# Down weights of two FFNs summed by POOL during the first up projection, and A split six blocks ahead

## The chip, the core and the metric

The kernel runs on one core of one Trainium2 chip. The metric is the device time of one execution in microseconds. Engines are named as the profile names them: PE (matmuls), PEld (PE's weight loads), DVE (the vector engine), ACT (the scalar engine), POOL (GpSimd), SP (the engine that only issues transfers).

## The reference, cut to what matters

Two transformer blocks follow each other on one sequence of 1024 tokens with 1024 features, in float32. Each ends with an FFN of hidden width 2816, and the change touches nothing else:

```python
# block 1
gate, up = jnp.split(xn @ w_gate_up[l], 2, axis=-1)
x = x + (jax.nn.silu(gate) * up) @ w_down[l]
# block 2
u = causal_dwconv(h @ w_ffn_up[l], w_ffn_conv[l])
gate, val = jnp.split(u, 2, axis=-1)
x = x + (jax.nn.silu(gate) * val) @ w_ffn_down[l]
```

## The kernel before, in words

**Precision.** A float32 product is made of three matmuls. Each operand is split into a rounded part "hi" (a copy on ACT, L256) and the rest "lo" (source minus hi on DVE, L257), and PE adds hi·hi, hi·lo and lo·hi (`mm3` at L267 to L269, `product` at L973).

**Up projections.** A unit f (1 to 21) makes 128 hidden features with one level of a Strassen scheme: 7 products of 4 row blocks, so 84 matmuls of 128x512. Its two raw weight blocks of 512 KB (u for up, g for gate) are loaded by SP (L129) into a ring of two raw buffers. Four slots per unit, a to d, are split from them; `add_unit` also forms sums of weight blocks in place on the raw buffers: S3 and S4 on DVE, S1 and S2 on POOL (L878). Slot b needs S3 and S1, slot c S2, slot d S4. A slot is split at most three slots ahead of the one in use, and u and g of the next unit are loaded when the raw buffer before them has been split. The finished hidden features (`sg`) go to DRAM (`hd`, L1059).

**Down projections.** The first 20 of the 22 hidden blocks are a 2x2 Strassen product: A (hidden features, from `hd`) times B (the down weights), in quadrants of 10 blocks. `DOWN` lists the seven products in order: A11·B11, A12·B21, S3·T3, A22·T4, S1·T1, S2·T2, S4·B22. S are sums of quadrants of A, T sums of quadrants of B (T3 = B22-B12, T1 = B12-B11, T2 = B11+T3, T4 = B21-T2). A product is 10 steps; a step is one k block of A for four token tiles, 12 matmuls into four PSUM banks. For every step one block of A must have been split (`operand`, tiles `ah`), in a ring of AR = 3, so three steps ahead at the most. The sums S are formed in `operand` (L1194). B11, B12 and B21 are loaded whole into SBUF at the start (L1142), B22 in pieces twice (L129), and `add_down` forms T3 and T1 on DVE and T2 and T4 on POOL (L845) right before the splits that use them. Finished banks are added to x by DVE (L980, `x<-dn,x`).

**The order of the work.** The program is written in one order, and a scheduler then places every instruction on its engine's queue by its own estimates of when it is ready; each engine runs its queue strictly in that order. So the order of a queue need not be that of the code. A transfer queued on SP behind another one that waits for its buffer waits too.

**Names that the prediction uses.** `wr` raw weights, `wh` and `wl` their split parts, `st` and `dn` PSUM banks of the up and the down projection, `a22` two buffers for quadrant A22, `sg` a finished hidden block, `pb` (new) POOL's ring of down weight blocks, `td` (new) the sums in DRAM.

Of the kernel before, what the change touches and what calls it, by code (L numbers as in the profile page):

```python
# [52 lines left out]
DE = dict(S3=pool_, T3=vec_, T1=vec_, T2=pool_, T4=pool_, S1=vec_, S2=vec_, S4=pool_)  # L53
# [104 lines left out]
class Kern:  # L158
# [6 lines left out]
    def setup(self):  # L165
        tc, nc = self.tc, self.nc
        self.const = c = tc.alloc_tile_pool(name="const", bufs=1)
        self.xnp = tc.alloc_tile_pool(name="xn", bufs=1)
        self.W = Weights(self, tc.alloc_tile_pool(name="w", bufs=1), 2, 3)
        self.dram = tc.alloc_tile_pool(name="dram", bufs=1, space=DRAM)  # L170
        self.hd = self.dram.tile([NF, P, S], F32, name="hd")
        self.ident = c.tile([P, P], F32, name="ident")
# [643 lines left out]
    def plan_ffn(self, which):  # L816
        a, W = self.a, self.W
        up = (a["w_gate_up"] if which == 1 else a["w_ffn_up_2"])[0].rearrange("(k p) c -> p k c", p=P)
        dn = (a["w_down"] if which == 1 else a["w_ffn_down_2"])[0].rearrange("(k p) c -> p k c", p=P)
        units, dw = {}, {}  # L820
        units[0] = [W.add([(0, up[:, :, o:o + P])], KT, P) for o in (0, DFF)]
        for f in range(1, NF):
            units[f] = self.add_unit(*[up[:, :, o + f * P:o + (f + 1) * P] for o in (0, DFF)])
        home, slots = {}, {}

        def rest():
            for f in range(2 * ND, NF):
                dw[f] = W.add([(0, dn[:, f:f + 1, :])], 1, D)

        for _, name in DOWN:  # L830
            if which == 1 and name == "T2":
                rest()
            for k in range(0, ND, 2):
                slots[name, k] = self.add_down(home, name, k, dn)
        if which == 2:
            rest()
        self.ffn_plan[which] = (units, home, slots, dn, dw)

    def add_down(self, home, name, k, dn):

        W, nc = self.W, self.nc
        raw = W.load([(0, dn[:, ND + k:ND + k + 2, 512:])], 2, 512) if name in ("T3", "B22") else None

        def tt(out, in0, in1, what):
            DE[what](nc).tensor_tensor(out=out, in0=in0, in1=in1, op=ALU.subtract)  # L845

        def make(hi, lo):
            out = []
            for j in range(2):
                h, l = (v[:, j * 512:(j + 1) * 512] for v in (hi, lo))  # L850
                b11, b12, b21 = (home.get((q, k + j)) for q in ("B11", "B12", "B21"))
                b22 = None if raw is None else W.raw[raw][:, j * 512:(j + 1) * 512]
                if name == "T3":
                    src = home["T3", j]
                    tt(src, b22, b12, "T3")
                    tt(b12, b12, b11, "T1")
                    tt(b11, b22, b12, "T2")
                else:
                    src = dict(B11=b11, B21=b21, T4=b21, T1=b12, T2=b11, B22=b22)[name]
                    if name == "T4":  # L860
                        tt(b21, b21, b11, "T4")
                self.split(h, l, src)
                out.append((h, l))
            return out
        return W.slot(make, raw)

    def add_unit(self, gate, up):
# [9 lines left out]
        def tt(name, in0, in1, op, what):  # L877
            SE[what](nc).tensor_tensor(out=raw(name), in0=raw(in0), in1=raw(in1), op=op)  # L878
# [63 lines left out]
    def ffn(self, which):  # L942
# [118 lines left out]
        def unit(f):  # L1061
# [32 lines left out]

            if f < NF - 1:
                second()
                third()
                flush(f - 1)
                add(v[:, main], b5, u2[:, main])
            else:  # L1100
                third()
                down_load()
                second()
                flush(f - 1)
                add(v[:, main], b5, u2[:, main])
                W.done(sb)
# [7 lines left out]
            add(u2[:, main], b5, u2[:, main])  # L1114
            if f == NF - 1:
                down_open()
# [19 lines left out]
        def fetch(q, k0, k1):  # L1136

            f = k0 + ND * ((q[2] if q[0] == "A" else q[1]) == "2")
            c = 512 * ((q[1] if q[0] == "A" else q[2]) == "2")
            src = self.hd[f:f + k1 - k0, :, c:c + 512].rearrange("k p c -> p k c") if q[0] == "A" else \  # L1140
                dn[:, f:f + k1 - k0, c:c + 512]
            nc.sync.dma_start(out=places[q, k0][:, :k1 - k0, :], in_=src)  # L1142
# [8 lines left out]
        def down_load():  # L1151

            for q, part in (("A11", "hi0"), ("B11", "lo0")):
                place(q, self.xnp.tile([P, KT, 512], F32, tag=part, name=q), 0, KT)
            for k in range(0, KT, 2):
                fetch("A11", k, k + 2)
                fetch("B11", k, k + 2)
# [3 lines left out]
        def down_open():  # L1161
# [7 lines left out]
            for j in range(2):  # L1169
                home["T3", j] = d.tile([P, 512], F32, name=f"T3{j}")  # L1170
            ring["a22"] = [d.tile([P, 512], F32, name=f"a22{i}") for i in range(A2)]
            for q in ("A11", "B11", "A21", "B12"):
                place(q, d.tile([P, ND - KT, 512], F32, name=f"{q}x"), KT, ND)
            for q, part in (("A21", "hi1"), ("B12", "lo1")):
                place(q, self.xnp.tile([P, KT, 512], F32, tag=part, name=q), 0, KT)
            fetch("A11", KT, ND)
            fetch("B11", KT, ND)
            fetch("A12", 0, ND // 2)
            fetch("A12", ND // 2, ND)
            for i in range(AR):  # L1180
# [39 lines left out]
        def load_rest():  # L1220

            dp.pop().release()
# [8 lines left out]
        def strassen():  # L1231
            pool.release()
            last = None
            d2 = tc.alloc_tile_pool(name=f"dr{which}", bufs=1, side="right", reuse_waits="tile")
            dp.append(d2)
            self.psum(dn=(1, 8))
            place("B21", d2.tile([P, ND, 512], F32, name="B21"), 0, ND)
            for q in ("B21", "A21", "B12"):
                cuts = ((0, ND // 2), (ND // 2, ND)) if q == "B21" else ((0, KT // 2), (KT // 2, KT), (KT, ND))
                for k0, k1 in cuts:  # L1240
                    fetch(q, k0, k1)
            for k in range(A2):
                load22(k)
            sums = []
            for i, (name, bname, k) in enumerate(steps):
# [14 lines left out]
                w = W.get(slots[bname, k - k % 2])[k % 2]  # L1260
# [20 lines left out]
            if which == 1:  # L1281
                W.done(slots[DOWN[-1][1], ND - 2])
            return last
# [3 lines left out]
        pool = tc.alloc_tile_pool(name=f"ffn{which}", bufs=1, side="right", reuse_waits="tile")  # L1287
        first(banks)
# [8 lines left out]
        else:  # L1297
# [3 lines left out]
            dp[1].release()  # L1301
# [956 lines left out]
```

## Time and profile before

| | |
|---|---|
| median of three runs | 2538.17 us (2536.41 to 2547.12) |
| the profiled execution | 2533.62 us |
| its span, first to last instruction | 2531.9 us |
| mean granted clock of PE, share of full speed | 0.986 |
| busy: PE, DVE, ACT, POOL | 96%, 73%, 45%, 18% |
| first up projection | about 500 to 950 us of the span |
| first down projection | about 950 to 1190 us |
| second up projection | about 1840 to 2285 us |
| second down projection | about 2285 to 2515 us |

The profile is of one execution. A busy PE is one with matmuls in its pipeline, so the number of matmuls in a stretch says more than its busy time. A group of instructions is told by its line, its engine and its tiles, and a line can be that of a helper which many stages call.

### The profile page before, as it was taken

How to read it: one execution, taken by the hardware profiler on the slowest of the kernel's cores; microseconds unless marked ns; L12 is line 12 of the kernel's file. 1: busy time of each engine (PE TensorE's matmuls, PEld its weight loads, DVE VectorE, ACT ScalarE, POOL GpSimd, SP SyncE). 2: the span in 40 equal slices, each digit the busy share in tenths (PEclk: the TensorE clock that was granted, in tenths of full speed). 3: DMA queues.
4: the chain of work that ended last, by engine and by line, in shares of the span. 5: the costliest groups of instructions: out<-in, count | busy, mean ns of one | idle time of the engine just before them, and what ended most of it. 6: DMA issues, size and time to landing. Idle time of an engine off the chain costs nothing. (4 is left out here: it accounts for less than half of the span.)

```text
span 2531.9 us, 33317 instructions
## 1 busy us (share of the span) xinstructions
PE 2420.6 (96%) x12360; PEld 1993.5 (79%) x12360; DVE 1856.3 (73%) x3342; ACT 1145.8 (45%) x2290; POOL 449.3 (18%) x412
## 2 busy tenths in 40 slices
PE   7999999999999999899999999989899999999898
PEld 7977779978888887678877777879678888887677
DVE  5557788655555557977777868777878788878977
ACT  5356675342232233337432434776744434434243
POOL 1000002031111114500210111332341111113600
PEclk9999999999999999899999999999999999999999
DMA  4110002112223236213211112131212222227202
GB/s 152 51 34 21 22 26 92 42 48 78 75 83 91 76 110 240 75 42 123 62 42 50 30 46 64 40 137 49 75 51 84 92 75 75 84 93 265 67 33 109
DMA packets 194675, 196.58 MB, mean 78 GB/s; under 512 B 11613, under 2 KB 154032, under 8 KB 194512
## 3 DMA queue, kind: packets, MB, share of 16 engines
q1 hardware_dynamic: 189760, 178.74, 22.2%
q0 software_dynamic: 4752, 15.71, 1.8%
q8 instruction: 97, 1.59, 0.3%
q14 instruction: 66, 0.54, 0.1%
HBM read 155.76 MB, written 38.67 MB: 77 GB/s over the span
## 5 line engine op out<-in xcount | busy, mean ns | idle before, releaser
L257 DVE TENSOR_TENSOR wl<-wr,wh 128x512 fp32r<-128x512 f32 (+4 forms) x388 | 300.9, 805 | 320.1 <-ACT wh L256 316.2
L256 ACT CAST wh<-wr 128x512 fp32r<-128x512 f32 (+4 forms) x388 | 257.2, 696 | 583.4 <-PE st L973 363.9
L269 PE MATMUL dn<-wh,ah 128*128 128x512 f32 x560 | 225.6, 403 | 21.6 <-DVE ah L257 21.6
L267 PE MATMUL dn<-wh,ah 128*128 128x512 f32 x560 | 226.0, 404 | 5.4 <-ACT ah L256 2.2
L268 PE MATMUL dn<-wl,ah 128*128 128x512 f32 x560 | 224.0, 400 | 0.0
L980 DVE TENSOR_TENSOR u<-st,u 128x512 f32<-128x512 f32 x260 | 168.0, 685 | 30.7 <-PE st L973 29.3
L878 POOL TENSOR_TENSOR wr<-wr 128x512 f32<-128x512 f32 x42 | 55.2, 1315 | 692.3 <-DVE wr L878 692.3
L269 PEld LDWEIGHTS dn<-wh,ah 128*128 128x128 f32 x560 | 107.3, 192 | 56.3 <-DVE ah L257 30.8
L973 PE MATMUL st<-f1hi,wl 128*128 128x512 f32 x368 | 147.2, 400 | 0.0
L973 PE MATMUL st<-f2hi,wl 128*128 128x512 f32 x368 | 147.1, 400 | 0.0
L973 PE MATMUL st<-f2lo,wh 128*128 128x512 f32 x368 | 147.0, 400 | 0.0
L973 PE MATMUL st<-f1lo,wh 128*128 128x512 f32 x368 | 146.6, 398 | 0.0
L973 PE MATMUL st<-f1hi,wh 128*128 128x512 f32 x368 | 145.2, 394 | 0.7 <-ACT f1hi L256 0.7
L973 PE MATMUL st<-f2hi,wh 128*128 128x512 f32 x368 | 145.0, 394 | 0.7 <-ACT f2hi L256 0.7
L267 PEld LDWEIGHTS dn<-wh,ah 128*128 128x128 f32 x560 | 107.4, 192 | 32.8 <-ACT ah L256 4.1
L268 PEld LDWEIGHTS dn<-wl,ah 128*128 128x128 f32 x560 | 107.5, 192 | 24.0
L256 ACT CAST ah<-A 128x512 fp32r<-128x512 f32 x104 | 63.7, 619 | 109.7 <-PE dn L268 94.7
L257 DVE TENSOR_TENSOR ah<-A,ah 128x512 fp32r<-128x512 f32 x104 | 82.4, 796 | 41.9 <-ACT ah L256 38.9
L973 PEld LDWEIGHTS st<-f2hi,wh 128*128 128x128 f32 x368 | 70.4, 191 | 17.3 <-ACT f2hi L256 0.9
L973 PEld LDWEIGHTS st<-f1hi,wh 128*128 128x128 f32 x368 | 70.4, 191 | 17.2 <-ACT f1hi L256 0.9
L973 PEld LDWEIGHTS st<-f2lo,wh 128*128 128x128 f32 x368 | 69.6, 189 | 16.0
L973 PEld LDWEIGHTS st<-f1lo,wh 128*128 128x128 f32 x368 | 69.4, 189 | 16.1
(547 smaller groups left out, 7079.8 us busy)
## 6 DMA issues: line engine op xcount, KB each, us to landing
wr<-in_w_gate_up_dram SPq DMA_DIRECT2D x44, 512.0 KB, 4.3
hd<-sg SPq DMA_DIRECT2D x44, 512.0 KB, 3.2
wr<-in_w_ffn_up_dram SPq DMA_DIRECT2D x44, 512.0 KB, 3.9
wr<-in_w_mix_in_dram SPq DMA_DIRECT2D x28, 512.0 KB, 4.0
wr<-in_w_in_dram SPq DMA_DIRECT2D x16, 512.0 KB, 3.9
wr<-in_w_down_dram SPq DMA_DIRECT2D x12, 512.0 KB, 3.3
wr<-in_w_ffn_down_dram SPq DMA_DIRECT2D x12, 512.0 KB, 3.3
A<-hd SPq DMA_DIRECT2D x4, 1280.0 KB, 14.3
```

The source lines that it names most:

```text
L256: self.nc.scalar.copy(hi, src)
L257: self.nc.vector.tensor_tensor(out=lo, in0=src, in1=hi.bitcast(F32), op=ALU.subtract)
L267: mm(out, a[0], b[0], start=start, stop=False)
L268: mm(out, a[0], b[1], start=False, stop=False)
L269: mm(out, a[1], b[0], start=False, stop=stop)
L878: SE[what](nc).tensor_tensor(out=raw(name), in0=raw(in0), in1=raw(in1), op=op)
L973: mm(ps, a[p][:, kk, :], b[q][:, kk, :], start=start and kk == 0 and j == 0, stop=kk == n - 1 and j == 2, skip_group_check=True)
L980: nc.vector.tensor_tensor(out=out, in0=ps, in1=t, op=ALU.add)
```

## The change

POOL forms T1 to T4 of both FFNs during the first up projection. `prepare_down` is a generator; each step of it is called at one of three places in a unit of the first FFN. For each of 20 k blocks (10 of each FFN) SP loads the four blocks B12, B22, B11, B21 (256 KB each) into the ring `pb` of six buffers, POOL makes the four sums in place and stores each (256 KB) to `td` by its own transfer queue: 80 loads, 80 sums, 80 stores. The down projections then take B11, B21, B22 and the T's as ordinary weights through the ring `wr`, 35 loads of 512 KB each, split as one piece of 128x1024. S1 and S2 of the units of the first FFN go from POOL to DVE; in the second FFN they stay. In the down projections S2 goes from DVE to POOL. The ring `ah` has six buffers: three (AR0) where the three were, and three in the memory that the up projection's pool leaves.

```diff
-ND, AR, A2, PB = 10, 3, 2, 2
+ND, AR, AR0, A2, PB = 10, 6, 3, 2, 2
-SE, TE, ME = dict(S3=vec_, S1=pool_, S2=pool_, S4=vec_), dict(T1=vec_, T2=pool_, T3=pool_, T4=pool_), vec_
+SE = {1: dict(S3=vec_, S1=vec_, S2=vec_, S4=vec_), 2: dict(S3=vec_, S1=pool_, S2=pool_, S4=vec_)}
-DE = dict(S3=pool_, T3=vec_, T1=vec_, T2=pool_, T4=pool_, S1=vec_, S2=vec_, S4=pool_)
+DE = dict(S3=pool_, S1=vec_, S2=pool_, S4=pool_)
...
-    def add_down(self, home, name, k, dn):
...
+    def add_down(self, which, name, k, dn):
+        f, c = k + ND * (name[1] == "2"), 512 * (name[2:] == "2")
+        return self.W.add([(0, dn[:, f:f + 2, c:c + 512] if name[0] == "B" else self.td[which, name][:, k:k + 2, :])],
+                          2, 512)
+
+    def prepare_down(self, pool):
+        nc = self.nc
+        for which in (1, 2):
+            dn = self.ffn_plan[which][3]
+            for k in range(ND):
+                def load(name):
+                    f, c = k + ND * (name[1] == "2"), 512 * (name[2] == "2")
+                    t = pool.tile([P, 512], F32, tag="pb", name="pb", bufs=6)
+                    nc.sync.dma_start(out=t, in_=dn[:, f, c:c + 512])
+                    return t
+                def keep(name, out, in0, in1, op):
+                    nc.gpsimd.tensor_tensor(out=out, in0=in0, in1=in1, op=op)
+                    nc.gpsimd.dma_start(out=self.td[which, name][:, k, :], in_=out)
+                b12, b22, b11, b21 = (load(n) for n in ("B12", "B22", "B11", "B21"))
+                yield
+                keep("T3", b22, b22, b12, ALU.subtract)
+                keep("T1", b12, b12, b11, ALU.subtract)
+                yield
+                keep("T2", b11, b11, b22, ALU.add)
+                keep("T4", b21, b21, b11, ALU.subtract)
+                yield
...
             product(b1, A12, "B21", False)
+            next(prep, None)
             if f < NF - 1:
                 second()
+                next(prep, None)
...
             add(u2[:, main], b5, u2[:, main])
+            next(prep, None)
...
-            ring["ah"] = [d.tile([P, 2, 512], F32R, name=f"ah{i}") for i in range(AR)]
+            ring["ah"] = [d.tile([P, 2, 512], F32R, name=f"ah{i}") for i in range(AR0)]
...
-            d2 = tc.alloc_tile_pool(name=f"dr{which}", bufs=1, side="right", reuse_waits="tile")
+            d = tc.alloc_tile_pool(name=f"dr{which}", bufs=1, side="right", reuse_waits="tile")
+            ring["ah"] += [d.tile([P, 2, 512], F32R, name=f"ah{i}") for i in range(AR0, AR)]
...
+            for i in range(AR0, AR):
+                operand(i)
```

**SP's queue in the first up projection.** `wr` are the raw weights of the units, two per unit, `hd<-sg` the store of a finished hidden block. Before:

```order
L129 DMA wr_5320<-in_w_gate_up_dram 128x8x128
L129 DMA wr_5640<-in_w_gate_up_dram 128x8x128
L1059 DMA hd<-sg 128x1024
L129 DMA wr_5970<-in_w_gate_up_dram 128x8x128
L129 DMA wr_6053<-in_w_gate_up_dram 128x8x128
L129 DMA wr_6118<-in_w_gate_up_dram 128x8x128
L1059 DMA hd<-sg 128x1024
L129 DMA wr_6159<-in_w_gate_up_dram 128x8x128
```

Now, from the same two loads (those of unit 1) on:

```order
L130 DMA wr_5328<-in_w_gate_up_dram 128x8x128
L130 DMA wr_5648<-in_w_gate_up_dram 128x8x128
L859 DMA pb<-in_w_down_dram 128x512 x11
L1067 DMA hd<-sg 128x1024
L130 DMA wr_5978<-in_w_gate_up_dram 128x8x128
L859 DMA pb<-in_w_down_dram 128x512 x4
L130 DMA wr_6069<-in_w_gate_up_dram 128x8x128
L859 DMA pb<-in_w_down_dram 128x512 x10
L130 DMA wr_6138<-in_w_gate_up_dram 128x8x128
L859 DMA pb<-in_w_down_dram 128x512
L1067 DMA hd<-sg 128x1024
L130 DMA wr_6183<-in_w_gate_up_dram 128x8x128
```

The 80 loads of `pb` do not stand four to a unit, as the code calls them. After the first 25 there follow 12 per unit (11 between g of one unit and u of the next, and one more), so that all 80 stand ahead of the raw weights of the units 2 to 8: 73 ahead of u of unit 7, 74 ahead of its g, 80 ahead of u of unit 8. From there on the queue is that of before.

**POOL's queue at the same place.** L878 are the sums of the units. Before:

```order
L878 TENSOR_TENSOR wr_5970<-wr_5970 128x512
L878 TENSOR_TENSOR wr_5970<-wr_5970,wr_6053 128x512
L878 TENSOR_TENSOR wr_6118<-wr_6118 128x512
L878 TENSOR_TENSOR wr_6118<-wr_6118,wr_6159 128x512
L878 TENSOR_TENSOR wr_6254<-wr_6254 128x512
```

Now, with buffer numbers:

```order
L863 TENSOR_TENSOR pb_6345<-pb_6345,pb_6343 128x512
L864 DMA td1T3_69<-pb_6345 128x512
L863 TENSOR_TENSOR pb_6343<-pb_6343,pb_6347 128x512
L864 DMA td1T1_67<-pb_6343 128x512
L863 TENSOR_TENSOR pb_6347<-pb_6347,pb_6345 128x512
L864 DMA td1T2_68<-pb_6347 128x512
L863 TENSOR_TENSOR pb_6349<-pb_6349,pb_6347 128x512
L864 DMA td1T4_70<-pb_6349 128x512
```

Two sums per unit have become sums and stores by turns, 80 of each in one run.

**DVE's queue in the first down projection.** Before, where steps 12 to 20 are prepared (`T` are the two buffers of T3, `B` quadrants of B):

```order
L845 TENSOR_TENSOR T_8857<-wr_8702,B_8866 128x512
L845 TENSOR_TENSOR T_8858<-wr_8702,B_8866 128x512
L257 TENSOR_TENSOR ah_8852<-A_8850,ah_8852 128x512
L257 TENSOR_TENSOR wl_9153<-B_8891,wh_9152 128x512 x2
L845 TENSOR_TENSOR B_8866<-B_8866,B_8777 128x512
L257 TENSOR_TENSOR ah_8853<-A_8850,ah_8853 128x512
L845 TENSOR_TENSOR B_8866<-B_8866,B_8777 128x512
```

Now, at the beginning of the same product A11·B11 (9174 to 9176 are the first three buffers of the ring, 9204 to 9206 the new ones):

```order
L261 TENSOR_TENSOR ah_9174<-A_9104,ah_9174 128x512
L261 TENSOR_TENSOR ah_9175<-A_9104,ah_9175 128x512
L261 TENSOR_TENSOR wl_9253<-wr_9146,wh_9252 128x1024
L261 TENSOR_TENSOR ah_9176<-A11x,ah_9176 128x512
L261 TENSOR_TENSOR ah_9204<-A_9104,ah_9204 128x512
L261 TENSOR_TENSOR ah_9205<-A_9104,ah_9205 128x512
L261 TENSOR_TENSOR ah_9206<-A_9104,ah_9206 128x512
```

The rows of L845 are gone, and a weight split is one row of 1024. The splits for steps 6, 7 and 8, which reuse the buffers of steps 0, 1 and 2, stand ahead of those for steps 3, 4 and 5; ACT's casts stand in the same order.

## Rows read from the trace of the kernel before

**Rows 1.** The page's first line.
```profile
span 2531.9 us, 33317 instructions
```

**Rows 2.** Busy time by stretch; PE, PEld, DVE, ACT, POOL, then clock, DMA share, GB/s.
```profile
600.00:940.00 340.00, 340.00 (x1466) 276.50 (x1466) 185.48 (x295) 97.81 (x173) 43.94 (x34) 1.00 0.28 84
...
1000.00:1080.00 80.00, 67.65 (x258) 51.03 (x257) 77.73 (x96) 25.91 (x45) 48.92 (x28) 0.91 0.20 66
2280.00:2300.00 20.00, 18.39 (x80) 14.68 (x79) 17.89 (x28) 12.28 (x22) 0.00 (x0) 1.00 1.03 372
2340.00:2420.00 80.00, 67.34 (x260) 50.55 (x260) 77.69 (x93) 26.18 (x47) 46.51 (x28) 0.94 0.20 66
```

**Rows 3.** PE's waits, the longest in total: us, times, longest.
```profile
PE dn L269 <- DVE ah L257: 21.6, 16, 2.9
```

**Rows 4.** The stretches of the two down projections, L845 alone: DVE, POOL.
```profile
1000.00:1080.00 80.00, 16.68 (x16) 35.54 (x19) 0.91 0.20 66
2340.00:2420.00 80.00, 15.59 (x15) 31.50 (x18) 0.94 0.20 66
```

**Rows 5.** DVE's groups by shape, 1000 to 1080 us: busy us, mean ns.
```profile
L257 DVE TENSOR_TENSOR ah<-A,ah 128x512 fp32r<-128x512 f32 x10 | 11.5, 1152 | 0.0
L980 DVE TENSOR_TENSOR x<-dn,x 128x512 f32<-128x512 f32 x16 | 10.5, 679 | 0.0
...
L1194 DVE TENSOR_TENSOR A<-a,A 128x512 f32<-128x512 f32 x8 | 6.5, 818 | 0.0
```

**Rows 6.** Timeline of DVE and of POOL there: start, us.
```profile
1019.42 1.77 DVE L257 TENSOR_TENSOR wl<-T,wh 128x512 fp32r<-128x512 f32 x1
1021.11 1.76 DVE L257 TENSOR_TENSOR ah<-A,ah 128x512 fp32r<-128x512 f32 x1
...
1023.99 0.68 DVE L845 TENSOR_TENSOR T<-wr,B 128x512 f32<-128x512 f32 x1
...
1019.02 1.61 POOL L845 TENSOR_TENSOR B<-B,B 128x512 f32<-128x512 f32 x1
```

**Rows 7.** POOL's groups by shape in the first up projection, 535 to 945 us.
```profile
L878 POOL TENSOR_TENSOR wr<-wr,wr 128x512 f32<-128x512 f32 x20 | 25.9, 1294 | 1.6
L878 POOL TENSOR_TENSOR wr<-wr 128x512 f32<-128x512 f32 x20 | 25.8, 1291 | 345.8 <-DVE wr L878 345.8
```

**Rows 8.** DVE's groups by shape in the first up projection, 650 to 940 us.
```profile
L257 DVE TENSOR_TENSOR wl<-wr,wh 128x512 fp32r<-128x512 f32 x105 | 68.4, 688 | 121.3 <-ACT wh L256 120.7
```

**Rows 9.** POOL's timeline: two issues of 256 KB stores.
```profile
1289.76 1.14 POOL L1870 DMA_DIRECT2D sqd<-sqt  x2 [28.36 <-ACT sqt L1869]
```

**Rows 10.** Transfers: KB each, median us to landing; the third of 1640 to 1700 us.
```profile
a<-hd SPq DMA_DIRECT2D x20, 256.0 KB, 2.7
sqd<-sqt POOLq DMA_DIRECT2D x8, 256.0 KB, 2.9
...
stage<-sqd SPq DMA_DIRECT2D x2, 256.0 KB, 3.7
wr<-in_w_gate_up_dram SPq DMA_DIRECT2D x44, 512.0 KB, 4.3
```

**Rows 11.** The eight stores of L1870 (sqd) alone.
```profile
DMA to landing us min/median/max: 2.4/2.9/5.6
```

**Rows 12.** Timeline of SP and of ACT around the beginning of unit 4.
```profile
581.87 0.34 SPq L1059 DMA_DIRECT2D hd<-sg  x1
582.51 4.00 SPq L129 DMA_DIRECT2D wr<-in_w_gate_up_dram  x2
601.38 0.34 SPq L1059 DMA_DIRECT2D hd<-sg  x1
...
582.16 0.59 ACT L1072 COPY u<-st 128x512 f32<-128x512 f32 x1 [1.32 <-PE st L973]
590.31 1.14 ACT L256 CAST wh<-wr 128x512 fp32r<-128x512 f32 x2 [4.92 <-PE st L973]
```

**Rows 13.** PE's timeline: the last transposes of the token tiles.
```profile
528.22 0.60 PE L921 MATMUL xT<-ident,xs 128*128 128x128 f32 x4
```

More of the change, by code (lines that the diff above doesn't have):

```diff
@@ L171, in setup @@
         self.hd = self.dram.tile([NF, P, S], F32, name="hd")
+        self.td = {(w, n): self.dram.tile([P, ND, 512], F32, name=f"td{w}{n}")
+                   for w in (1, 2) for n in ("T1", "T2", "T3", "T4")}
         self.ident = c.tile([P, P], F32, name="ident")
@@ L822, in plan_ffn @@
         for f in range(1, NF):
-            units[f] = self.add_unit(*[up[:, :, o + f * P:o + (f + 1) * P] for o in (0, DFF)])
+            units[f] = self.add_unit(which, *[up[:, :, o + f * P:o + (f + 1) * P] for o in (0, DFF)])
         home, slots = {}, {}
@@ L837, in plan_ffn @@
         self.ffn_plan[which] = (units, home, slots, dn, dw)
-    def add_down(self, home, name, k, dn):
[L841 to L865, printed above, removed]
@@ L869, in add_unit @@
+    def add_unit(self, which, gate, up):
         W, nc = self.W, self.nc
@@ L877, in tt @@
         def tt(name, in0, in1, op, what):
-            SE[what](nc).tensor_tensor(out=raw(name), in0=raw(in0), in1=raw(in1), op=op)
+            SE[which][what](nc).tensor_tensor(out=raw(name), in0=raw(in0), in1=raw(in1), op=op)
         def cut(hi, lo, *names):
@@ L1151, in down_load @@
         def down_load():
-            for q, part in (("A11", "hi0"), ("B11", "lo0")):
-                place(q, self.xnp.tile([P, KT, 512], F32, tag=part, name=q), 0, KT)
+            place("A11", self.xnp.tile([P, KT, 512], F32, tag="hi0", name="A11"), 0, KT)
             for k in range(0, KT, 2):
                 fetch("A11", k, k + 2)
-                fetch("B11", k, k + 2)
         ring = {}
@@ L1165, in down_open @@
             place("A12", d.tile([P, ND, 512], F32, name="A12"), 0, ND)
-            ring["ah"] = [d.tile([P, 2, 512], F32R, name=f"ah{i}") for i in range(AR)]
+            ring["ah"] = [d.tile([P, 2, 512], F32R, name=f"ah{i}") for i in range(AR0)]
             d = tc.alloc_tile_pool(name=f"dm{which}", bufs=1, reuse_waits="tile")
             dp.append(d)
-            for j in range(2):
-                home["T3", j] = d.tile([P, 512], F32, name=f"T3{j}")
             ring["a22"] = [d.tile([P, 512], F32, name=f"a22{i}") for i in range(A2)]
-            for q in ("A11", "B11", "A21", "B12"):
+            for q in ("A11", "A21"):
                 place(q, d.tile([P, ND - KT, 512], F32, name=f"{q}x"), KT, ND)
-            for q, part in (("A21", "hi1"), ("B12", "lo1")):
-                place(q, self.xnp.tile([P, KT, 512], F32, tag=part, name=q), 0, KT)
+            place("A21", self.xnp.tile([P, KT, 512], F32, tag="hi1", name="A21"), 0, KT)
             fetch("A11", KT, ND)
-            fetch("B11", KT, ND)
             fetch("A12", 0, ND // 2)
             fetch("A12", ND // 2, ND)
-            for i in range(AR):
+            for i in range(AR0):
                 operand(i)
@@ L1287, in ffn @@
         pool = tc.alloc_tile_pool(name=f"ffn{which}", bufs=1, side="right", reuse_waits="tile")
+        prep = self.prepare_down(pool) if which == 1 else iter(())
         first(banks)
@@ L1300, in ffn @@
             down(range(2 * ND, NF), self.tail2())
-            dp[1].release()
+            for d in dp[:0:-1]:
+                d.release()
     def tail1(self):
```

23 lines of the change are left out of this document (9 added, 14 removed).

## Prediction

> **What bounds the kernel now.** I read the span first [rows 1], then busy time by stretch, then what PE waits for, then the groups and the order of time in the stretches where PE loses. In the first up projection PE loses nothing: 1466 matmuls are recorded in 340 us, 0.232 us each, at full clock (2.4 GHz), with DVE busy 55% of the time, POOL 13% and the transfers 28% [rows 2]. PE loses in the down projections. At that rate 80 us hold 345 matmuls; 1000 to 1080 us has 258 and 2340 to 2420 us has 260, so 172 are missing, 39.9 us. At the start of the second down projection (2280 to 2300 us) 6 of 86 are missing, 1.4 us. Together 41.3 us. In the two long stretches DVE is busy 97% of the time and the granted clock sinks to 0.91 and 0.94 [rows 2]. PE's longest wait in total is for the lo half of a split of A, 21.6 us in 16 waits [rows 3]; the rest of the loss is the lower clock and waits that the profile shows in smaller groups. So there DVE is the bound.
>
> Part of DVE's time is POOL's. A DVE instruction that reads two SBUF tiles takes 0.68 us alone, and 1.76 to 1.77 us when POOL's sum runs beside it, which itself takes 1.61 us [rows 6] and not 1.29 us [rows 7]. DVE's adds from PSUM into x are not hurt: 679 ns in the same stretch, where the splits of A take 1152 ns on the mean [rows 5]. Two-tile work of DVE and sums of POOL go one after the other.
>
> **What the change takes from the down projections.** The T sums go: 16 instructions and 16.7 us of DVE and 19 and 35.5 us of POOL in the first stretch, 15.6 and 31.5 us in the second [rows 4]. S2 goes from DVE to POOL, 10 per projection at 0.82 us [rows 5], some 8 us of DVE. Of DVE's 77.7 us [rows 2] 53 are left, for matmuls that at full rate take 258 x 0.232 = 60 us. DVE is then no longer the bound on the mean, and six blocks of lead (6 x 12 x 0.232 = 16.7 us) stand where there were three. At the beginning the loads of A no longer share the queue with those of B, which removes the 1.4 us.
>
> Two things remain late. First, the splits for the steps 6, 7, 8 stand on ACT and on DVE ahead of those for 3, 4, 5 (the last order rows). The split for step 8 needs the buffer that step 2 reads, so step 3 can only begin after step 2 has ended and two casts (1.14 us for two [rows 12]) and one subtraction (0.69 us [rows 8]) have followed; with some 0.1 us for each handover that is a hole of 2.1 us in each down projection. Second, in A22·T4 POOL has S2 and S4 by turns, 20 sums or 25.8 us at 1.29 us [rows 7]; DVE has 10 splits of A, 5 of weights and 10 sums, some 18 us at 0.6 to 0.7 us per 512 columns. In a row they take 43.8 us, against ten steps of 27.8 us and the lead of 16.7 us. That just fits; I leave 1 us per projection. Gain: 41.3 - 4.2 - 2 = 35 us, with 41.3 as one bound and as the other 19 us (half of the lead already spent when that product begins, 8 us lost in each).
>
> The 70 splits of 1024 columns instead of 140 of 512 cost nothing: ACT and DVE have the time. 35 loads of 512 KB per down projection need one per 5.6 us, and such loads land in 4.3 us [rows 10].
>
> **What it adds in the first up projection.** S1 and S2 come to DVE: 40 at 0.69 us, 1.4 us per unit, hidden in its 45% idle time [rows 2, 7, 8]. POOL gets 80 sums at 1.29 us and 80 issues of a store at 0.57 us (1.14 for two [rows 9]), in one row. Between a sum and its store, and between a store and the next sum, I add 0.08 us together, and for DVE's two-tile instructions 0.1 us: DVE has 13 of them per unit (7 splits, 4 sums, 2 of sg), 0.6 us each, so a sum meets one in a third of cases and waits half of it. That is 2.04 us per sum.
>
> It matters because of SP's queue. The raw weights of the units 2 to 8 stand behind loads of `pb`, and such a load waits until POOL has summed and stored what was in its buffer (ring of six). Twelve of them per unit need 12 x 2.04 = 24.5 us, and a unit takes 19.5 us (two stores of sg, 581.87 to 601.38 [rows 12]). So PE is late at every unit until the 80 are through. What that adds up to is read from g of unit 7, which stands behind 74 loads. The 74th needs the buffer of the 68th, so 68 sums must be done. POOL can begin once the memory of the token tiles is free, after the transposes at 528.2 us [rows 13], and a first pair has landed, 2.7 us [rows 10] and two issues later: 532.5 us. The last store lands in 2.9 us [rows 10], with 0.6 us for two issues. g of unit 7 is then issued at 532.5 + 68 x 2.04 + 3.5 = 674.7 us. Before, g of unit 4 was issued at 586.1 (the end of the second load at 582.51 [rows 12]), that of unit 7 three units later, at 644.6: it is 30.1 us late. The slack: before, it lands after 4.3 us [rows 10] at 590.4, is split by 591.7, and unit 4 begins at 598.9 (unit 3 began 12 matmuls before the copy at 582.16 [rows 12], at 579.4). So 7.2 us are free, and the loss is 22.9 us; in general 68 x pace - 115.8. With u of unit 8 the queue is free, and nothing gives the time back.
>
> Bounds of the pace: below, 1.86 us, sum and issue alone (loss 10.7). Above, the ring: T1 of a block needs B11 in the buffer from which T1 of the block before has been stored, so four sums take at least one sum, one store and one load to land, and a handover of 0.2 us. With 2.9 and 2.7 us [rows 10] that is 7.1 us or 1.78 per sum, less than POOL's own 2.04. With the slowest store, 5.6 us [rows 11], and the load at a busier time, 3.7 us [rows 10], it is 10.8 us or 2.70 (loss 67.8). I take 2.04, since a load and a store of just these sizes are at 2.7 and 2.9 us in the rows; but those were taken at a light load. The transfers themselves need 24 x 256 KB at 372 GB/s, 16.9 us per unit, and 28% of 19.5 us for the rest [rows 2], together 22.4 us or 1.87 per sum, close below POOL.
>
> The Trainium skill has a rule against this (DMA: Bandwidth & Descriptors, Latency and other measured facts): access to HBM takes 0.2 us on the mean and 2 us at high load. By it, as an estimate, both transfers would take 1.8 us more, the pace 2.67 us, and the time 2569 us. The trace bears it out in part: 3.7 us against 2.7 us for a load of the same size [rows 10]; in rival A, whose upper bound has nearly the same pace from rows alone, this end has a fifth of the chance.
>
> **The sum.** 22.9 - 35 = -12.1 us on the profiled execution's 2533.6 us, 2521.5. The median of the three runs stands 4.6 us above that execution, so 2526 us.
>
> **The rivals.**
> *A, slower: the ring's transfers set POOL's pace.* The point from which the change loses is a pace of 2.22 us (68 x 2.22 - 115.8 = 35), reached when store and load both land in 3.7 us. Between that and the upper bound, at 2.46, the loss is 51.5 us: 2554 us, and 2571 at the bound. For it: transfers at 22.4 us per unit against POOL's 24.5 leave little room, and SP waits in order. Against it: at most six blocks are under way.
> *B, no change:* A22·T4 or the first steps give back half of the gain (19 us), as two-tile work of DVE still meets POOL there: 22.9 - 19 = +4, 2542 us. Against it: the lead has doubled.
> *C, clearly faster:* the queue is hidden better, pace 1.86 and no loss left in A22·T4: 10.7 - 37.1 = -26 us, 2512 us. Against it: the order of POOL's queue lets no sum overlap a store's issue.
> That a DVE bound takes over in the up projection I do not count apart: 13 two-tile instructions at 1.76 us [rows 6] and 7 adds at 0.69 are 27.7 us per unit at the very worst, and it would show as a case of A.
>
> **How the numbers follow.** Half a percent is 12.7 us, about what a measurement of this kernel can tell from no change. Forecast 44%, own range 2517 to 2537 us (pace 1.94 to 2.14, gain 31 to 37), which lies on both sides of the bound: 26 faster, 18 same. A 24%, all slower. B 18%: 15 same, 3 slower. C 14%, all faster. So faster 40%, same 33%, slower 27%. The range leaves out the end of C and the worst of A: 2503 to 2566 us.
>
> **What would show it.** Right: from about 555 to 680 us PE waits at the head of each unit for casts that wait for `wr`, SP's loads of `wr` stand behind `pb`, and POOL has a sum and a store every 2.04 us with no idle time; after unit 8 units of 19.5 us; the down stretches at 4.2 to 4.3 matmuls per us, but for a hole at step 3. Wrong: POOL idle for transfers and a pace above 2.2 us (A); DVE still busy over 90% in the down stretches (B); no wait at the units (C).

## The result, and the profile after

The changed kernel takes 2598.05 us (median of four runs, 2591.41 to 2607.59), against 2537.47 us for the kernel before on the same chip: ratio 1.0229, 95% interval 1.0206 to 1.0252. It is 2.3% slower; the forecast was 2526 us.

Five moments of PE's timeline divide the span: the first `dn` matmul, the first `svab` matmul (the tail's first product), the first matmul of the second up projection (`st<-f2hi`), the second first `dn` matmul, and the end.

| stretch, us | before | after | difference | forecast |
|---|---|---|---|---|
| start to the first down projection | 949.5 | 1037.8 | +88.2 | +22.9 |
| first down projection | 242.5 | 228.0 | -14.4 | -35, both together |
| second block up to its up projection | 644.6 | 651.5 | +6.9 | 0 |
| second up projection | 448.9 | 448.9 | -0.1 | 0 |
| second down projection, end | 246.4 | 234.8 | -11.6 | (above) |
| span | 2531.9 | 2600.9 | +69.0 | -12.1 |

Busy time by stretch in the kernel after (length, then PE, PEld, DVE, ACT, POOL, the clock, the DMA share, GB/s), to be held against [rows 2]:

```profile
540.00:740.00 200.00, 128.47 (x500) 102.08 (x499) 143.11 (x112) 33.62 (x59) 144.13 (x155) 0.81 0.74 246
760.00:940.00 180.00, 180.00 (x777) 146.43 (x776) 112.36 (x179) 52.83 (x95) 0.00 (x0) 1.00 0.25 79
1080.00:1160.00 80.00, 78.30 (x338) 63.10 (x337) 71.78 (x77) 30.53 (x43) 35.78 (x21) 1.00 0.40 125
```

While POOL makes its sums (535.6 to 741.5 us), PE does 2.5 matmuls per us where it did 4.3 before, and the granted clock is 0.81. From 760 us on the unit runs as before. Nearly the whole loss lies in those 200 us: before, they hold 863 matmuls, now 500, and 363 at 0.232 us each are 84 us. Another 2.8 us are a wait of PE at the first `dn` matmul, which the kernel before does not have. In the third row the down projection does 338 matmuls in 80 us where [rows 2] has 258.

SP's waits in the kernel after, 535 to 760 us (us in total, times, longest):

```profile
SPq L130 <- DVE wr L886: 60.8, 8, 15.1
SPq L859 <- DMA td1T<-pb: 57.5, 25, 6.3
SPq L859 <- DMA td2T<-pb: 40.5, 15, 7.5
SPq L859 <- POOL pb L863: 15.6, 16, 2.5
```

PE's waits in the same stretch:

```profile
PE st L981 <- DVE u L988: 58.6, 5, 15.2
PE st L981 <- ACT wh L260: 13.0, 1, 13.0
```

The first line decides against the mechanism forecast: at the raw weights (L130) SP stands waiting for DVE's S4, 8 times (four times for 6.9 to 7.4 us between 587 and 719 us; the two longest waits come behind the last `pb`). SP was early at them, not late behind `pb`. Once it was late as forecast: the raw weights issued at 560.14 stood behind four `pb` transfers that had waited 6.1 us for the ring, and PE's wait of 13.0 us for a cast follows. At the heads of the later units PE waits for DVE's adds out of its banks.

One unit of the kernel after, by the engines' timelines (start, us, then the instruction). SP:

```profile
587.54 1.06 SPq L130 DMA_DIRECT2D wr<-in_w_gate_up_dram  x1
588.70 23.27 SPq L859 DMA_DIRECT2D pb<-in_w_down_dram  x11
619.20 0.38 SPq L130 DMA_DIRECT2D wr<-in_w_gate_up_dram  x1
```

ACT, the first casts of that unit:

```profile
595.33 1.14 ACT L260 CAST wh<-wr 128x512 fp32r<-128x512 f32 x2 [10.98 <-DMA wr<-in_w_gate_up_dram]
```

DVE:

```profile
595.98 2.36 DVE L261 TENSOR_TENSOR wl<-wr,wh 128x512 fp32r<-128x512 f32 x2 [8.47 <-ACT wh L260]
598.26 2.23 DVE L886 TENSOR_TENSOR wr<-wr,wr 128x512 f32<-128x512 f32 x1
600.53 3.31 DVE L886 TENSOR_TENSOR wr<-wr 128x512 f32<-128x512 f32 x1
603.76 0.68 DVE L988 TENSOR_TENSOR u<-st,u 128x512 f32<-128x512 f32 x1
...
606.09 1.87 DVE L988 TENSOR_TENSOR u<-st,u 128x512 f32<-128x512 f32 x3
...
617.49 1.65 DVE L886 TENSOR_TENSOR wr<-wr,wr 128x512 f32<-128x512 f32 x1
```

PE, its first matmul after the gap:

```profile
606.91 0.77 PE L981 MATMUL st<-f1hi,wh 128*128 128x512 f32 x1 [15.15 <-DVE u L988]
```

POOL:

```profile
596.04 1.75 POOL L863 TENSOR_TENSOR pb<-pb 128x512 f32<-128x512 f32 x1 [5.35 <-DMA pb<-in_w_down_dram]
598.09 0.56 POOL L864 DMA_DIRECT2D td1T<-pb  x1 [0.30 <-POOL pb L863]
598.66 1.27 POOL L863 TENSOR_TENSOR pb<-pb 128x512 f32<-128x512 f32 x1
```

Read in order of time. The gate's weights are issued at 587.54 and followed by eleven `pb` transfers. They are there at 595.3, 7.8 us later. Then DVE makes `wl`, S3 and S1, and in its queue these stand ahead of the adds out of the banks. Beside POOL's sums S3 takes 2.23 and S1 3.31 us instead of 0.69. The adds come at 603.8 and 606.1, PE starts at 606.91 after 15 us, at first at the low clock (0.77 us for a matmul that takes 0.39 on the median). S4 ends at 619.1, and at once SP issues the next raw weights. It is a loop through DVE: late S4, late weights, late S4. POOL, which was to set the pace, had itself waited 5.35 us for a `pb` issued behind those weights.

Its transfers, 560 to 740 us (KB each, median us to landing), against [rows 10]:

```profile
pb<-in_w_ffn_down_dram SPq DMA_DIRECT2D x40, 256.0 KB, 4.3
td2T<-pb POOLq DMA_DIRECT2D x39, 256.0 KB, 3.2
td1T<-pb POOLq DMA_DIRECT2D x29, 256.0 KB, 3.8
...
wr<-in_w_gate_up_dram SPq DMA_DIRECT2D x11, 512.0 KB, 6.3
```

Its DVE groups by shape, 535 to 740 us (busy us, mean ns), against [rows 8]:

```profile
L261 DVE TENSOR_TENSOR wl<-wr,wh 128x512 fp32r<-128x512 f32 x44 | 63.1, 1463 | 55.5 <-ACT wh L260 47.6 <-PE st L981 7.9
L886 DVE TENSOR_TENSOR wr<-wr,wr 128x512 f32<-128x512 f32 x18 | 35.0, 1947 | 0.0
...
L886 DVE TENSOR_TENSOR wr<-wr 128x512 f32<-128x512 f32 x6 | 17.6, 2932 | 0.2
```

So two suspects are left, both at work in the same stretch: DVE's two-tile instructions beside POOL's sums, and raw weights that land in 6.3 us instead of 4.3.

### The profile page after: what moved, and what is told of

Read it like the earlier page. It is cut to its first block, busy times and chain, and to the rows that moved or that the text cites. A ratio compares the mean times of both kernels' runs of the same rounds, so it can differ in the third digit from the quotient of the medians.

```text
span 2600.9 us, 33630 instructions
## 1 busy us (share of the span) xinstructions
PE 2429.8 (93%) x12360; PEld 2006.7 (77%) x12360; DVE 1924.0 (74%) x3254; ACT 1138.2 (44%) x2220; POOL 512.5 (20%) x510
## 5 line engine op out<-in xcount | busy, mean ns | idle before, releaser
L261 DVE TENSOR_TENSOR wl<-wr,wh 128x512 fp32r<-128x512 f32 (+3 forms) x438 | 418.6, 979 | 329.8 <-ACT wh L260 316.7
L260 ACT CAST wh<-wr 128x512 fp32r<-128x512 f32 (+3 forms) x438 | 319.2, 756 | 715.0 <-PE st L981 389.5
L271 PE MATMUL dn<-wh,ah 128*128 128x512 f32 x560 | 223.4, 399 | 5.4 <-DVE u L988 3.3
L273 PE MATMUL dn<-wh,ah 128*128 128x512 f32 x560 | 222.8, 398 | 2.3 <-DVE ah L261 2.2
L981 PE MATMUL st<-f1hi,wh 128*128 128x512 f32 x368 | 151.1, 411 | 71.5 <-DVE u L988 58.6
L1197 POOL TENSOR_TENSOR A<-A,A 128x512 f32<-128x512 f32 x32 | 56.8, 1791 | 352.9 <-PE dn L272 310.1
L863 POOL TENSOR_TENSOR pb<-pb 128x512 f32<-128x512 f32 x80 | 106.0, 1329 | 45.4 <-DMA pb<-in_w_ffn_down_dram 22.2
L886 POOL TENSOR_TENSOR wr<-wr 128x512 f32<-128x512 f32 x21 | 27.1, 1292 | 346.6 <-DVE wr L886 346.6
L886 DVE TENSOR_TENSOR wr<-wr,wr 128x512 f32<-128x512 f32 x105 | 94.4, 899 | 0.1
```

Of the source, the lines that this page charges most:

```text
L260: self.nc.scalar.copy(hi, src)
L261: self.nc.vector.tensor_tensor(out=lo, in0=src, in1=hi.bitcast(F32), op=ALU.subtract)
L271: mm(out, a[0], b[0], start=start, stop=False)
L273: mm(out, a[1], b[0], start=False, stop=stop)
L863: nc.gpsimd.tensor_tensor(out=out, in0=in0, in1=in1, op=op)
L886: SE[which][what](nc).tensor_tensor(out=raw(name), in0=raw(in0), in1=raw(in1), op=op)
```

## The experiments

The number to watch is the time of the first `dn` matmul, 949.5 us before and 1037.8 after. It is read from the profiled execution. The times are medians of several executions in the change and the runs 2, 6 and 9, and of one execution in the others.

**1. No preparation.** The raw quarters are loaded in place of the sums; S1 and S2 stay on DVE.

```
-        prep = self.prepare_down(pool) if which == 1 else iter(())
+        prep = iter(())
```

> The changed kernel without its preparation: nothing is summed or stored in the first up projection, and the down projections load raw quadrants where the T sums would be (so the T's are left out). Theory L (the loss comes from the 80 loads that stand in SP's queue ahead of the raw weights, in a loop with POOL and DVE): the first up projection ends as in the kernel before, near 950 us of the span instead of 1038, and the whole is some 2515 us (before, less the 26 us that the two down projections gained, plus up to 7 us that the changed kernel lost between them). Rival M (a good part of the loss is the new memory layout and DVE's unit sums, with or without the preparation): first up projection still over 970 us, whole over 2535 us.

Measured: 2516.77 us, first `dn` at 951.2, first down stretch 227.8, `svab` to the second up projection 654.7. The whole loss comes from the preparation; rival M is out. What the sums would be worth if they were free is seen too: 20 us (the kernel before takes 2536.91 us on that chip). And 10 us are lost between the FFNs without any preparation.

**2. Four transfers per unit**, held in SP's queue behind the unit's last raw weights.

```
+                    self.tc.add_manual_dep(ins.ins, self.W.last.ins.name, NOSYNC, reason="four per unit")
```

> The changed kernel, with the loads of pb held in SP's queue behind the raw weights of the unit in which the code calls them: four per unit over 20 units instead of twelve per unit over seven. The same 80 loads, sums and stores. Theory L: POOL needs 4 x 2.16 = 8.6 us of a unit's 19.5, no raw weight is late, the first up projection ends near 955 us, the whole is some 2518 us, ratio to before near 0.992. Rival P (POOL's sums and DVE's two-tile instructions exclude each other, and that alone costs PE): the same number of collisions, so much the same loss: end of the first up projection beyond 1000 us, the whole over 2565 us. Rival T (the transfers are saturated): a third of the load per unit, no loss, as theory L.

Measured: 2625.12 us, ratio 1.0345 (1.0305 to 1.0385); first `dn` at 1057.0. SP never stood at `pb` ahead of raw weights, and it was worse. My first theory, the queue, falls; the rival P, which put it above 2565 us, is borne out in the time.

**3. The stream without POOL's sums** (loads and stores as in the change, raw quarters stored).

```
-                    nc.gpsimd.tensor_tensor(out=out, in0=in0, in1=in1, op=op)
```

> The changed kernel with loads and stores of pb, but without POOL's 80 sums (raw blocks are stored, the T's are left out). Theory L: the pace is set by the ring's transfers, about 2.0 to 2.2 us per load instead of 2.57, the queue is still too long for a unit (12 x 2.1 = 25 us), and the end of the first up projection comes near 985 us instead of 1038; whole near 2548 us. Rival P (exclusion of POOL and DVE alone): no sums, no loss: end near 955 us, whole near 2518 us. Rival T (transfers alone): same traffic, so end near 1030 us, whole near 2595 us.

Measured: 2574.6 us, first `dn` at 1007.0, on none of the three values. Of the 88 us 57 are there without a single sum. Its busy time, 560 to 680 us:

```profile
560.00:680.00 120.00, 79.48 (x305) 63.30 (x306) 47.72 (x76) 23.10 (x40) 35.23 (x65) 0.80 0.97 334
```

Its waits of ACT, 535 to 760 us:

```profile
ACT wh L260 <- DMA wr<-in_w_gate_up_dram: 76.6, 8, 15.6
```

The transfer engines are busy 97% of the time at 334 GB/s. But the wait of up to 15.6 us is not all theirs. The head of one unit, SP, DVE's S4, and ACT's first cast:

```profile
618.23 28.98 SPq L859 DMA_DIRECT2D pb<-in_w_ffn_down_dram  x17
647.31 0.39 SPq L130 DMA_DIRECT2D wr<-in_w_gate_up_dram  x1
648.83 0.45 SPq L130 DMA_DIRECT2D wr<-in_w_gate_up_dram  x1
...
640.46 0.68 DVE L885 TENSOR_TENSOR wr<-wr,wr 128x512 f32<-128x512 f32 x1
...
659.72 1.14 ACT L260 CAST wh<-wr 128x512 fp32r<-128x512 f32 x2 [15.56 <-DMA wr<-in_w_gate_up_dram]
```

S4 ends at 641.14, but SP is still at `pb` and issues the next raw weights only at 647.31, 6.2 us later; that is the forecast mechanism. The gate's weights, issued at 648.83, are cast at 659.72, 10.9 us later, where 4.3 us to landing are usual. So this run has two causes in about equal parts, the queue and the full transfer engines. It does not stand for the change without its sums: the stream runs faster in it (334 GB/s against 246), and the queue, which delays each of these units, delayed one load in the change. What it shows for the change is that the stream, run without a limit, can fill the transfer engines.

**4. Unit sums on DVE alone**, in the kernel before.

```
-SE, TE, ME = dict(S3=vec_, S1=pool_, S2=pool_, S4=vec_), dict(T1=vec_, T2=pool_, T3=pool_, T4=pool_), vec_
+SE = {1: dict(S3=vec_, S1=vec_, S2=vec_, S4=vec_), 2: dict(S3=vec_, S1=pool_, S2=pool_, S4=vec_)}
+TE, ME = dict(T1=vec_, T2=pool_, T3=pool_, T4=pool_), vec_
```

> The kernel before with one part of the change alone: S1 and S2 of the first FFN's units on DVE. Theory L: 1.4 us per unit in DVE's idle time, no change, 2531 to 2537 us. Rival M: these sums stand ahead of the adds from PSUM in DVE's queue and make PE wait also without POOL: 5 us or more slower.

Measured: 2542.66 us, first `dn` at 955.5. In the units the move costs nothing: from 560 to 940 us there are 1639 matmuls, as before. Of the 6.0 us by which `dn` is later 4.2 are a wait of PE at the first `dn` for DVE, and the time lies within the spread of the kernel before on that chip (2533.17 to 2545.41).

**5 to 7. Why four per unit lost.** Three edits of run 2: without the sums (run 5); with the sums put behind S4, where DVE is nearly idle (run 6, whose edit is shown in part); and with S1 and S2 back on POOL (run 7).

```
+                    self.tc.add_manual_dep(ins.ins, self.gate.ins.name, NOSYNC, reason="behind S4")
...
+                self.gate = nc.gpsimd.tensor_copy(out=gate, in_=self.s4[:, 0:1])
```

> Four transfers of 256 KB per unit behind the unit's last weights, as in the run with four per unit (first `dn` matmul at 1057.0 us, 2625 us), but POOL's additions and subtractions left out (what is stored is the raw quarter). Collision theory (the sums start 5 us behind the gate's weights, just when DVE makes S3, S1 and S2; the two lengthen each other, the additions out of PSUM stand behind S1 in DVE's queue, PE waits 3 us and then runs at half clock): the loss goes, first `dn` at 952 to 965 us, 2515 to 2530 us; DVE's S3 and S1 back at 0.69 us each instead of 1.8 and 2.1. Transfer theory (1 MB behind the gate's 512 KB makes these late; ACT's casts waited for `wr` 48.6 us in 9 units): the waits of ACT for `wr` stay at 4 to 6 us per unit, first `dn` above 1020 us, over 2580 us.

> Four per unit with S1 and S2 of the first FFN on POOL again, as in the kernel before. If the loss came from giving the unit sums to VectorE, it goes: dn near 955 us, 2520 us. Collision theory: S3 on DVE still falls on a sum, and S1 now stands behind or between POOL's sums (2.16 us each with the store's issue), so the second pair of operands is later, not earlier: dn at 1040 to 1090 us, 2600 to 2660 us.

> Four per unit again, with the sums of a unit held on POOL behind DVE's S4 of that unit (a copy of one column of S4's result goes ahead of them; their transfers were issued a unit earlier), so that their 8.6 us lie between S4 and the next S3, where the run without preparation has DVE nearly idle for 9.9 us. Collision theory: S3, S1, S2 at 0.69 us but for the one that the last sum overlaps; first `dn` at 953 to 970 us; the end at 2517 to 2535 us, so 0.5% faster than before at best and equal at worst. Transfer theory: no better than four per unit, first `dn` above 1020 us, over 2580 us. Theory that any sum on POOL costs DVE wherever it lies: `wl`, `sg` and the copies stretched, dn at 980 to 1020, 2545 to 2585 us.

Measured without the sums (run 5): 2523.45 us, first `dn` at 961.6. DVE's groups of run 2, 560 to 940 us:

```profile
L887 DVE TENSOR_TENSOR wr<-wr,wr 128x512 f32<-128x512 f32 x47 | 60.0, 1276 | 0.0
L887 DVE TENSOR_TENSOR wr<-wr 128x512 f32<-128x512 f32 x15 | 29.6, 1974 | 0.5
```

The same groups of this run:

```profile
L886 DVE TENSOR_TENSOR wr<-wr,wr 128x512 f32<-128x512 f32 x58 | 39.6, 683 | 0.0
...
L886 DVE TENSOR_TENSOR wr<-wr 128x512 f32<-128x512 f32 x19 | 13.1, 692 | 0.7
```

The same transfers in the same places of SP's queue, and raw weights that land in 4.5 us on the median in both; only the sums are gone, and with them 95 of the 107 us. That is the first cause, the collision: in a unit of run 2 ACT casts the gate's weights at 672.84, POOL has its `pb` and begins to sum at 674.26, DVE begins S3 at 674.71, and the adds that free PE's banks stand behind S3 and S1. PE waits 53.0 us for such adds from 560 to 940 us, without the sums 3.5.

With S1 and S2 back on POOL (run 7): 2591.22 us, first `dn` at 1024.0, below my range of 1040 to 1090. It is 33 us better than run 2, but 74 of the 107 us stay, where the theory of the moved unit sums wanted 955. Giving these sums to DVE adds to the collision; it is not its cause.

With the sums behind S4 (run 6): 2587.67 us, ratio 1.0191 (1.0166 to 1.0216), first `dn` at 1017.3. S3, S1 and S2 are at 0.69 us, as the collision theory says, and the forecast of 2517 to 2535 is missed all the same. ACT's waits for the raw weights there, 560 to 950 us:

```profile
ACT wh L260 <- DMA wr<-in_w_gate_up_dram: 130.4, 17, 9.0
```

POOL's stores, now begun at S4, and the `pb` transfers meet the gate's weights, which are issued 5 us after S4 and needed as soon as they land. First `dn` lies in the range of the third theory (980 to 1020 us), and in part that theory holds: the splits `wl`, which now meet the sums, take 818 ns on the mean, where the kernel before has 688 [rows 8].

**8. No preparation, three blocks of A ahead.**

```
-ND, AR, AR0, A2, PB = 10, 6, 3, 2, 2
+ND, AR, AR0, A2, PB = 10, 3, 3, 2, 2
```

> The run without preparation (raw quarters loaded in place of the sums, 2516.8 us, first down stretch 227.8 us, before 242.5) with three blocks of A split ahead in place of six. If the six blocks bring the gain of the down projections, the stretch goes back to 236 to 242 us; if it comes from the four subtractions and their stalls that left DVE and POOL, it stays within 2 us of 228 and the hole at step 3 (1.0 us) goes. I expect 228 to 231 us and 2515 to 2522 us.

Measured: 2514.22 us, first down stretch 227.9. The six blocks bring nothing that is seen. The gain belongs to what else the change does there: the T sums taken from DVE and POOL, S2 moved from DVE to POOL, the weights loaded in pieces. No run separates these.

**9 to 12. The collision and the transfers beside the gate's weights taken away.** With the sums behind S4, two shifts: the transfers of `pb` held until the next unit's first `wl` (the gate's weights have landed by then), and the four sums in one block with the four stores behind them.

```
+                    lo = W.parts[units[f + 1][0]][0][1]
+                    nc.gpsimd.tensor_copy(out=t[:, 0:1], in_=lo.bitcast(F32)[:, 0, 0:1])
...
+                for name, out, *_ in sums:
+                    last = after(nc.gpsimd.dma_start(out=self.td[which, name][:, k, :], in_=out), last)
```

> Sums behind S4 as before it (2587.7 us, where ACT waited for late `wr` 130.4 us in 17 units: the gate's weights landed 5.6 us after their issue, beside 1 MB of `pb` and the stores, and without preparation 4.2 us), with two more shifts: the four transfers of `pb` are held behind the gate's weights of the next unit (a column of that unit's `wl` is copied into each first), and the four sums run as one block with the four stores behind them. Theory that exactly two things cost the time, sums on DVE's pair S3/S1 and transfers on the gate's weights: both are gone, ACT's waits for `wr` fall below 1 us per unit, first `dn` at 951 to 962 us, the end at 2512 to 2530 us, ratio 0.990 to 0.997. Rival, that sums on POOL slow DVE's other work (`wl`, `sg`) enough to hold PE: dn at 975 to 1010 us, 2540 to 2575 us.

> Only the first of the two shifts: the transfers of `pb` held behind the next unit's first `wl`, sums behind S4 with a store after each (8.6 us). If the transfers made the gate's weights late: ACT's waits for `wr` under 2 us per unit, the last sum may meet the next `wl` and S3 (up to 1 us per unit); dn at 955 to 980 us, 2520 to 2545 us. If it was the stores: dn stays at 1000 to 1020 us.

> Only the second of the two shifts: sums as one block behind S4, stores behind them, but the transfers of `pb` straight behind the gate's weights. If the transfers of `pb` make the gate's weights late: still 4 to 7 us waits of ACT for `wr` in each unit, dn at 1000 to 1020 us, 2570 to 2590 us. If it was the stores beside them: dn near 955 us, 2520 us.

> What the run with one block of sums was meant to be: sums in one block behind S4 with the four stores behind them, and the transfers of `pb` directly behind the gate's weights (there they had come to stand between the up and the gate weights, so that they landed after S4 and the sums fell on S3 again). If both the transfers of `pb` and the stores beside the gate's weights make these late, as 2587.7 us with neither shift and 2555.4 us with the transfers held alone suggest: ACT still waits 4 to 7 us for `wr` in each unit, first `dn` at 985 to 1012 us, 2545 to 2582 us. If the stores alone do it: dn at 953 to 962 us, 2515 to 2525 us.

| first `dn`, us (time) | stores between the sums | stores behind the block |
|---|---|---|
| `pb` behind the gate's weights | 1017.3 (2587.67) | 964.0 (2533.25) |
| `pb` held until `wl` | 996.1 (2555.38) | 953.0 (2518.33) |

Run 10 is not in the table: in it the `pb` transfers came to stand between the up and the gate weights, landed after S4, and POOL's block fell on S3 again (first `dn` at 1017.7, 2580.83 us). It is one more case of the collision. Run 12 is the cell that it was meant to be, and it hit neither of my ranges (985 to 1012, and 953 to 962 if the stores alone do it), but came close to the second: grouping is worth 53 us, or 43 with the transfers held; holding the transfers 21 us, and 11 once the sums are grouped. I had taken the held run (2555) as a sign that both weigh alike.

Grouping moves more than the stores. The split `wl` behind S4 frees the gate's raw buffer; beside sums and stores by turns it meets a sum, as a rule, and in the block it does not wait (run 11, then run 9):

```profile
658.45 1.52 DVE L261 TENSOR_TENSOR wl<-wr,wh 128x512 fp32r<-128x512 f32 x1 [2.36 <-ACT wh L260]
644.47 0.69 DVE L261 TENSOR_TENSOR wl<-wr,wh 128x512 fp32r<-128x512 f32 x1 [2.38 <-ACT wh L260]
```

So the gate's weights are issued 4.67 us after the up weights in the median unit of runs 6 and 11, and 3.86 us after them in runs 12 and 9. From their issue to the cast they take 6.1 and 5.5 us in runs 6 and 11, 4.8 and 4.1 in runs 12 and 9. Of the 2.1 to 2.2 us per unit that grouping brings, 0.8 are again the collision on DVE, and 1.3 to 1.4 are the transfers.

With both, the kernel takes 2518.33 us against 2542.28: ratio 0.9911 (0.9895 to 0.9926). It beats both kernels. Its busy time, 560 to 940 us:

```profile
560.00:940.00 380.00, 378.96 (x1633) 307.65 (x1632) 236.12 (x370) 109.33 (x194) 198.29 (x252) 1.00 0.57 188
```

Its DVE groups of unit sums there:

```profile
L896 DVE TENSOR_TENSOR wr<-wr,wr 128x512 f32<-128x512 f32 x58 | 39.6, 682 | 0.0
...
L896 DVE TENSOR_TENSOR wr<-wr 128x512 f32<-128x512 f32 x19 | 13.1, 692 | 0.7
```

POOL's timeline in one unit (S4 ends at 641.3, the next S3 starts at 651.30):

```profile
641.36 0.19 POOL L870 COPY pg<-wr 128x1 f32<-128x1 f32 x1 [8.12 <-DVE wr L896]
641.50 6.18 POOL L878 TENSOR_TENSOR pb<-pb 128x512 f32<-128x512 f32 x4
647.62 2.17 POOL L880 DMA_DIRECT2D td1T<-pb  x4
```

POOL's group of sums:

```profile
L878 POOL TENSOR_TENSOR pb<-pb 128x512 f32<-128x512 f32 x80 | 119.1, 1489 | 4.7
```

The same 80 sums, 80 loads and 80 stores as in the change, spread over 20 units and put between S4 and the next S3: PE is busy 379 of 380 us, and S3, S1, S2 take what they take alone.

## Why the prediction was wrong

**The loss in the first up projection: +88.2 us, not +22.9.** Three steps failed.

The step "hidden in its 45% idle time", for DVE. I charged the meeting of two-tile instructions to POOL alone, as 0.1 us per sum, and looked at DVE's share of busy time. What counts is the place: S3 and S1 stand between the landing of the weights and the adds that free PE's banks. I even had the number: 27.7 us of DVE per unit "at the very worst", 8 us above the unit's 19.5, and set it aside as a case of A. Runs 2 and 5 are the test: of the 107 us that run 2 loses 95 go with the sums, at equal transfers. The Trainium skill (SBUF — State Buffer, Who interferes with whom) says that a DVE instruction with two SBUF inputs and a POOL instruction that reads SBUF exclude each other, and that the order of issue decides who waits. The trace agrees: in the change DVE pays (S1 at 2.93 us on the mean), in the last version POOL does (1489 ns per sum where [rows 7] have 1291 ns, DVE's `wr` sums at 0.68).

The step on the transfers, "22.4 us or 1.87 per sum, close below POOL". I used it as a limit of POOL's pace only. 22.4 us in a unit of 19.5 also means that the transfer engines have no room left while the stream lasts, and the unit's own weights go through them: in the change, whose units have grown to some 32.5 us, the engines are 74% busy and the weights land in 6.3 us on the median instead of 4.3; in run 3, without sums, they are 97% busy and a gate's weights take 10.9 us to the cast.

The step "PE is late at every unit" because raw weights "stand behind loads of `pb`" whose buffers wait for POOL. But for one load, SP waited at the raw weights for S4, so the queue was not the bound; with the queue cut to four per unit (run 2) the loss grew. POOL's pace was worse than the 2.04 us at which I had set it: 2.16 in a row (the sum 1.29, a handover of 0.30 before the store's issue of 0.55, where I had put 0.08 for both), and 2.57 on the mean from 535.6 to 741.5 us, with the waits for `pb`. With 2.57 the formula 68 x pace - 115.8 gives 59 us and still misses the 88, since what it describes is not what happened. Rival A had the sign and a part of the mechanism (transfers slower than at light load), not the place.

The rule that the prediction took from the Trainium skill (DMA: Bandwidth & Descriptors, Latency and other measured facts), up to 2 us of access time at high load, pointed the right way: `pb` landed in 4.0 to 4.3 us instead of 2.7, the stores in 3.2 to 3.8 instead of 2.9. Its price belonged on the raw weights as well.

**The gain in the down projections: 26.0 us, not 35.** The mechanism was right: the stretch of 80 us that had 258 matmuls has 338, with the T sums gone from DVE and POOL. Run 8 shows that the lead of six blocks, which the forecast had beside it, was not needed for the gain. What was mis-sized is the rest that stays. PE's waits in the first down projection of the kernel after (1037 to 1266 us):

```profile
PE dn L271 <- DVE u L988: 2.8, 1, 2.8
PE xT L327 <- DVE x L988: 2.1, 1, 2.1
PE dn L272 <- DVE wl L261: 1.7, 1, 1.7
PE dn L271 <- ACT ah L260: 1.0, 1, 1.0
```

The last is the hole at step 3, sized at 2.1 us and found at 1.0; but behind it the clock falls, and 1037 to 1057 us has 69 matmuls at 0.91 where the next 20 us have 88. The third costs 8 matmuls more (80 in 20 us). I had 3.1 us left over per projection for both; with the wait at the end (2.1 us, 0.5 before) it is some 7.5. In the second down projection two places cost more: 2366 to 2386 us has 61 matmuls and 2466 to 2486 us 70, where the other 20 us between 2366 and 2586 us have 87 to 89.

**Nothing between the FFNs: +6.9 us.** From `svab` to the second up projection it took 644.6 us before and 651.5 after. PE's queue is the same there in all kernels. DVE's differs from that before at a few places in the first norms, but it is the same in runs 1, 6, 9 and in the change, and these took 654.7, 645.3, 651.7 and 651.5 us. Up to 174 us in, before and run 1 agree within 0.5 us; then PE waits 2.4 us for the same DVE instruction in both, and afterwards run 1 is 3.2 us behind. The 25 us from 175 us on, before:

```profile
1367.00:1392.00 25.00, 22.59 (x131) 18.71 (x130) 11.71 (x26) 4.22 (x6) 2.13 (x5) 0.93 0.22 67
```

And run 1:

```profile
1354.00:1379.00 25.00, 22.62 (x118) 18.85 (x117) 12.23 (x29) 4.21 (x6) 2.14 (x5) 0.80 0.11 32
```

Equal busy time, 131 matmuls against 118: after the same wait PE runs longer at the low clock. At this place the difference is the clock's. Run 1 falls behind at two more places, by 2.3 us up to 281 us in and by 4.6 us up to 376 us in; the granted clock is lower there too (0.82 against 1.00 over 18 us from 264 us on, 0.83 against 0.94 over 30 us from 348 us on), but what PE waited for there was not followed up. What decides how long the clock stays low is open.

## What to carry to other kernels

Before giving an idle engine a side job, look at where in each period its instructions and transfers will fall, not at busy shares: here 80 sums and 160 transfers delayed the first `dn` by 88 us when run as fast as they can and by 3.5 us when held to one slot per unit. Keep POOL's sums away from the DVE two-tile instructions that stand between a landing and a freed PSUM bank or raw buffer, and bulk transfers away from the one load that has no slack. A worst case that exceeds the period ("27.7 us per unit" against 19.5) is a rival of its own with a price, and not a footnote.

## What the runs showed of the hardware

- Between a POOL sum and the issue of its store 0.30 us pass. Four sums and four stores by turns take 9.1 us (run 11, 655.50 to 664.60) and begin the first store 2.2 us after the end of S4; as a block they take 8.3 us (run 9, 641.50 to 649.79) and begin it after 6.3 us. In the block the sums take 1489 ns on the mean and DVE's `wl` beside them 0.75 us on the median; by turns `wl` takes some 1.6 us.
- A 512 KB load of raw weights landed in 4.5 to 5.5 us on the median of runs 2, 5, 6, 10, 11 and 12 instead of 4.2 to 4.3, though the transfer engines were busy only about half of the time there. The mean share does not tell which: run 9 has 4.2 us at 57%, run 6 has 4.8 us at 49%.
- The same wait of 2.4 us at the same instruction was followed by stretches at the low clock of different length (0.93 and 0.80 over 25 us), and the work between the FFNs, the same in four kernels, took between 645.3 and 654.7 us.
